# An encoder layer on one core: the rotation of q and k on VectorE, their turning amid other products, and a triangular substitution in three places

## The chip, the cores and the metric

The kernel runs on one core of a Trainium2 chip. The metric is device microseconds of one execution; lower is better. A core has TensorE (matrix products, PE in the views), VectorE (DVE), ScalarE (ACT), GpSimd (POOL), SyncE (SP, which here only issues DMAs) and 16 DMA engines that share its queues.

## The reference, cut to what matters

One layer of a hybrid encoder: x is 512 tokens by 1024. Two branches start from the same normalised h. Branch A is an RWKV-7 time mixing with a scan in both directions, branch B a differential attention. Both are gated and summed, then follow a feed-forward part and a second gate. The change touches branch B and a preparation of branch A's scan.

```python
q = partial_rope(q, cos, sin) * (DH ** -0.5)   # first 16 of each head's 64 are rotated
k = partial_rope(k, cos, sin)
...
def block(q_blk):
    s = jnp.einsum('bhcqd,bhckd->bhcqk', q_blk, kt).astype(f32)
    pr = jax.nn.softmax(s, axis=-1)
    pd = pr[:, :, 0] - lam * pr[:, :, 1]
    return jnp.einsum('bhqk,bhkv->bhqv', pd.astype(vt.dtype), vt)
...
o = o * lax.rsqrt(jnp.mean(o * o, axis=-1, keepdims=True) + SUBLN_EPS)
```

The scan of branch A (`state*w - ... + v*k`, 512 steps) is done in chunks of 64 tokens. Each chunk needs the inverse of a unit triangular 64x64 matrix; there are 128 of them (8 chunks, 8 heads, 2 directions), one to a partition.

## The kernel before

Every fp32 product is made of three products of rounded halves (`whi`/`wlo` of a weight, `hhi`/`hlo` of the activation), so a product is 3 matmuls a tile. A weight unit comes by DMA into `raw`; ScalarE rounds it to `whi`, VectorE (now and then GpSimd) forms `wlo`. The halves stand in a ring of four, the raw units in a ring of three.

The span goes through these stages: branch A's preparation, up to about 192 us; q, k and v of branch B (tiles `da`), up to 257; the attention loop, 17 turns, up to 320; the norm of its result, the corner blocks of the inverses and the branch's output product (`yb`), up to 382; branch A's scan, up to 486; then the output product, the feed-forward part and the last gate, up to the end.

**q, k, v.** For b = 0, 1, 2 (q, k, v) `dense_tm` makes two token tiles of 128 tokens at a time, 48 matmuls a pair. ScalarE scales each tile out of PSUM into `qk`; GpSimd rotates it (six operations of 128x64 for each token tile: L842 to L847, through the tile `rt`); TensorE turns it, 16 transposes of 128x128 into the four banks `qt` (L852); ScalarE and VectorE split each bank into halves (`qhl`, `kh`, `kl`).

**The loop.** Of each turn t: scores (`sc`), their largest value (`mx`), exponentials (`e`), the weighing of the two maps (GpSimd adds, VectorE scales by `s`), turning by TensorE (`tp`), the two halves of the turned tile (`turned_h` on ScalarE, `turned_l`, which is `pdTl` on VectorE), and the products with v (`ov`). Between them stand *fills*, three matmuls each: seven gates of eight fills into the banks `gA`, whose result `go` VectorE and ScalarE form, and then 32 fills of `yb`. There are two banks for gates: gate n+2 gets the bank of gate n once the `go` of gate n has been read out of it.

**The substitution.** `diag_blocks()` loads 2 MB into the tile `mi` (128 matrices, one to a partition) and inverts the two 32x32 diagonal blocks of each by 30 steps, s = 1 to 30. A step is two VectorE operations of 2*s*(31-s) elements a partition: 60, 116, 168, ... up to 480 at s = 15 and 16, and down again to 60. Then `mi` is stored to `td`, and four copies by ScalarE (`tr`) to `trd`. `corner_blocks()` loads both back (`u`, `bd`) and forms the off-diagonal block by four groups of 32 small matmuls (`iv`), which the scan needs.

**What sets the order.** `K(f, ...)` chains the operations of one engine in the order in which they are written; `chained` does so for TensorE. What isn't chained is put in order by a scheduler. `SUBS` says how many substitution steps are written ahead of q's, k's and v's products and in each turn of the loop, `CT` the turn in which the corner loads are written, `C0` the number of fills between the norm and the first `iv`.

Of the kernel before, what the change touches and what calls it, by code (L numbers as in the profile page):

```python
# [10 lines left out]
F32 = mybir.dt.float32  # L11
# [98 lines left out]
class Weights:  # L110
# [44 lines left out]
def tile_hybrid_encoder(ctx, tc, xT, wts, par, cst_a, cst_p, lor, lqk, nfin, out, dbg=None):  # L155
# [413 lines left out]
    AFS = [1, 1, 1, 1, 1, 1, 1, 1, 1, 1, 1, 1, 1, 2, 3, 3, 3]  # L569
# [47 lines left out]
    def diag_blocks():  # L617

        inv = pool("inv", side="right")
        mi = inv.tile([P, 2, H * (C + 1)], F32, name="mi")
        mif = mi.rearrange("u b x -> u (b x)")
        nc.sync.dma_start(mif[:, 0:C * C], md.rearrange("u s t -> u (s t)"))
        mfull = mif[:, 0:C * C].rearrange("u (s t) -> u s t", t=C)
        mb = mi[:, :, 0:H * C].rearrange("u b (s t) -> u b s t", t=C)
        tr = at.tile([P, H, H], F32, tag="pdTl", name="tr0", bufs=2)
        tmpo = inv.tile([P, 2 * 240], F32, name="tmpo")
        with tc.issue_after(W.last[0].ins):
            nc.scalar.activation(tr, mfull[:, 0:H, H:].rearrange("u s t -> u t s"), AF.Copy)  # L630
        nc.sync.dma_start(trd[:, 0], tr)
        for s in range(1, H - 1):
            n = H - 1 - s
            t_ = tmpo[:, 0:2 * s * n].rearrange("u (b i j) -> u b i j", b=2, j=n)
            with tc.issue_after(W.last[1].ins):
                nc.vector.tensor_tensor(t_, mb[:, :, 0:s, s:s + 1].broadcast_to([P, 2, s, n]),
                                        mb[:, :, s:s + 1, s + 1:H].broadcast_to([P, 2, s, n]), ALU.mult)
# [12 lines left out]
        nc.sync.dma_start(trd[:, 1], tr)  # L650
        inv.close_()
# [146 lines left out]
    for b in range(3):
        w = [W.next("intok", 1920 + 512 * b, k2) for k2 in range(4)]
        if b == 0:  # L800
            diag = diag_blocks()
        for _ in range(SUBS[b]):
            next(diag)
        if b < 2:
            qk = at.tile([P, 4, 8, 64], F32, tag="qk", name=f"qk{b}", bufs=1)
        pss_ = []
        for pair in range(2):
            for j in range(2):
                if pair == 0:
                    ps = psd.tile([P, 512], F32, tag="d", name=f"da{b}{j}")  # L810
                elif b < 2:
                    ps = psm.tile([P, 512], F32, tag="sc", name=f"da{b}{2 + j}", bufs=4)
                else:
                    ps = psm.tile([P, 512], F32, tag=("tp", "ov")[j], name=f"da{b}{2 + j}", bufs=1)
                pss_.append(ps)
            if b == 2 and pair == 1:
                for t in range(2):
                    scores(t)
                    exps(t)
                weigh(0)  # L820
            if last_pe is None:
                dense_tm(w, pss_[2 * pair:], 2 * pair, hhi, hlo)
            else:
                with tc.issue_after(last_pe.ins):
                    last_pe = dense_tm(w, pss_[2 * pair:], 2 * pair, hhi, hlo)
        for tt in range(4):
            ps = pss_[tt]
            if b < 2:
                nc.scalar.activation(qk[:, tt], ps.rearrange("p (h e) -> p h e", e=64), AF.Copy, scale=(rsq if b == 0 else rsx)[:, tt:tt + 1])
            else:  # L830
                nc.scalar.activation(vh[:, tt, :], ps, AF.Copy, scale=rsx[:, tt:tt + 1])
                nc.vector.scalar_tensor_tensor(vl[:, tt, :], ps, rsx[:, tt:tt + 1], vh[:, tt, :].bitcast(F32), ALU.mult, ALU.subtract)
        if b == 2:
            continue
        cos = ca[:, CA["cos"]:CA["cos"] + 32].rearrange("p (t e) -> p t e", e=8)
        sin = ca[:, CA["sin"]:CA["sin"] + 32].rearrange("p (t e) -> p t e", e=8)
        for tt in range(4):
            rt = at.tile([P, 4, 8, 8], F32, tag="rt", name=f"rt{b}{tt}", bufs=2)
            x1, x2 = qk[:, tt, :, 0:8], qk[:, tt, :, 8:16]
            cb = cos[:, tt, None, :].broadcast_to([P, 8, 8])  # L840
            sb = sin[:, tt, None, :].broadcast_to([P, 8, 8])
            nc.gpsimd.tensor_tensor(rt[:, 0], x1, cb, ALU.mult)  # L842
            nc.gpsimd.tensor_tensor(rt[:, 1], x2, sb, ALU.mult)
            nc.gpsimd.tensor_tensor(rt[:, 2], x2, cb, ALU.mult)
            nc.gpsimd.tensor_tensor(rt[:, 3], x1, sb, ALU.mult)
            nc.gpsimd.tensor_tensor(x1, rt[:, 0], rt[:, 1], ALU.subtract)
            nc.gpsimd.tensor_tensor(x2, rt[:, 2], rt[:, 3], ALU.add)  # L847
        dump("q" if b == 0 else "kq", qk)
        for hd in range(4):
            ps = psm.tile([P, T], F32, tag="sc", name=f"qt{b}{hd}", bufs=4)  # L850
            for tt in range(4):
                nc.tensor.transpose(ps[:, tt * P:(tt + 1) * P], qk[:, tt, 2 * hd:2 * hd + 2, :].rearrange("p h e -> p (h e)"), ident)  # L852
            for c in range(2):
                rows, other = slice(C * c, C * c + C), slice(C - C * c, P - C * c)
                dh = (qhl if b == 0 else kh2)[:, hd, c, :]
                nc.scalar.activation(dh[rows], ps[rows], AF.Copy)
                if b == 1:
                    nc.scalar.activation(dh[other], ps[rows], AF.Copy)
                dl = dh[other] if b == 0 else kl[rows, hd, c, :]
                nc.vector.tensor_tensor(dl, ps[rows], dh[rows].bitcast(F32), ALU.subtract)  # L860
# [52 lines left out]
    for t in range(NT + 1):  # L913
        if t > 2:
            values((t - 3) // 2, (0, 1) if t % 2 == 1 else (2, 3))
        if t + 3 < NT:
            scores(t + 3)
        fillk(AFS[t] if done < AFT else 0, True)
        if t > 0:
            turned_h(t - 1)  # L920
        if t + 2 < NT:
            exps(t + 2)
        if t + 1 < NT:
            weigh(t + 1)
# [557 lines left out]
```

## Time and profile before

| | |
|---|---|
| median of 3 runs | 973.64 us (965.7 to 975.59) |
| the profiled execution | 966.75 us, of which its span 964.8 us |
| TensorE busy | 888.8 us, 92% of the span |
| VectorE, ScalarE, GpSimd busy | 592.4, 450.5, 102.8 us |
| mean granted TensorE clock | 0.969 |

The span's busy time is 92% TensorE's. Granted clock is a share of 2.4 GHz. A row of a timeline gives start, duration, engine, line, operation and tiles; in brackets stands the idle time of that engine just before it and what ended it. L578 (and L667 in TensorE's rows) is the line in `K` (in `chained`), so operations recorded there are told apart by their tiles.

### The profile page before, as it was taken

How to read it: one execution, taken by the hardware profiler on the slowest of the kernel's cores; microseconds unless marked ns; L12 is line 12 of the kernel's file. 1: busy time of each engine (PE TensorE's matmuls, PEld its weight loads, DVE VectorE, ACT ScalarE, POOL GpSimd, SP SyncE). 2: the span in 40 equal slices, each digit the busy share in tenths (PEclk: the TensorE clock that was granted, in tenths of full speed). 3: DMA queues.
4: the chain of work that ended last, by engine and by line, in shares of the span. 5: the costliest groups of instructions: out<-in, count | busy, mean ns of one | idle time of the engine just before them, and what ended most of it. 6: DMA issues, size and time to landing. Idle time of an engine off the chain costs nothing.

```text
span 964.8 us, 14347 instructions
## 1 busy us (share of the span) xinstructions
PE 888.8 (92%) x5672; PEld 756.8 (78%) x5672; DVE 592.4 (61%) x885; ACT 450.5 (47%) x708; POOL 102.8 (11%) x139
## 2 busy tenths in 40 slices
PE   5899899987879998879999999999999999999996
PEld 4778777766767786668887788888888888888885
DVE  7766999667998632336889665554345335435453
ACT  7765555445578633213174454543234224313555
POOL 5000000144242141113200000000000000000000
PEclk9999999988989999889899999999999999999998
DMA  6343878742114468988524622333333332333512
GB/s 230 118 155 137 284 262 272 258 174 88 65 77 114 116 168 292 276 270 247 172 66 142 206 90 94 103 109 91 105 110 94 103 109 90 108 109 90 185 53 88
DMA packets 67859, 142.80 MB, mean 148 GB/s; under 512 B 26064, under 2 KB 28368, under 8 KB 65488
## 3 DMA queue, kind: packets, MB, share of 16 engines
q1 hardware_dynamic: 63696, 120.38, 38.5%
q0 software_dynamic: 4096, 21.50, 7.5%
q8 instruction: 45, 0.74, 0.3%
q14 instruction: 22, 0.18, 0.1%
HBM read 108.83 MB, written 33.03 MB: 147 GB/s over the span
## 4 chain that ended last, share of the span: by engine, by line
PE 61%; DVE 19%; DMA 7%; ACT 7%; issue 3%; POOL 2%; SPq 0%; DVEq 0%; ACTq 0%
PE f L247 11%; PE f L248 11%; PE f L246 11%; DMA ybt<-ybd 3%; PE gA L667 3%; DVE wlo L135 2%; DVE ga L520 2%; PE ss L1011 1%; DMA ybd<-yo 1%; PE wout L247 1%; PE wout L246 1%; PE wout L248 1%; DVE mx L578 1%; PE yy L1011 1%; PE yb L667 1%
## 5 line engine op out<-in xcount | busy, mean ns | idle before, releaser
L131 ACT ACTIVATE whi<-raw 128x1024 fp32r<-128x1024 f32 x134 | 141.4, 1056 | 282.8 <-PE f L247 182.8
L135 DVE TENSOR_TENSOR wlo<-raw,whi 128x1024 fp32r<-128x1024 f32 x131 | 163.2, 1247 | 51.6 <-ACT whi L131 51.4
L248 PE MATMUL f<-fh,wlo 128*128 128x512 f32 x256 | 97.2, 380 | 0.0
L246 PE MATMUL f<-fh,whi 128*128 128x512 f32 x256 | 97.1, 379 | 0.0
L247 PE MATMUL f<-fl,whi 128*128 128x512 f32 x256 | 97.1, 379 | 0.0
L247 PE MATMUL f<-h1l,whi 128*128 128x512 f32 x256 | 97.0, 379 | 0.0
L246 PE MATMUL f<-h1h,whi 128*128 128x512 f32 x256 | 97.0, 379 | 0.0
L248 PE MATMUL f<-h1h,wlo 128*128 128x512 f32 x256 | 97.0, 379 | 0.0
L1261 DVE TENSOR_TENSOR x<-x,f 128x512 f32<-128x512 f32 x32 | 22.0, 687 | 89.5 <-PE f L248 89.5
L1250 DVE SCALAR_TENSOR_TENSOR ft<-f,rf 128x512 f32<-128x512 f32 x32 | 22.1, 691 | 63.1 <-PE f L248 63.1
L246 PE MATMUL in<-hhi,whi 128*128 128x512 f32 x128 | 50.0, 391 | 6.6 <-ACT whi L131 6.6
L248 PEld LDWEIGHTS f<-h1h,wlo 128*128 128x128 f32 x256 | 48.4, 189 | 6.9
L247 PEld LDWEIGHTS f<-h1l,whi 128*128 128x128 f32 x256 | 48.4, 189 | 6.9
L246 PEld LDWEIGHTS f<-h1h,whi 128*128 128x128 f32 x256 | 48.4, 189 | 6.9
L246 PEld LDWEIGHTS f<-fh,whi 128*128 128x128 f32 x256 | 48.4, 189 | 6.8
L247 PEld LDWEIGHTS f<-fl,whi 128*128 128x128 f32 x256 | 48.4, 189 | 6.8
L248 PEld LDWEIGHTS f<-fh,wlo 128*128 128x128 f32 x256 | 48.4, 189 | 6.8
L247 PE MATMUL in<-hlo,whi 128*128 128x512 f32 x128 | 50.2, 392 | 1.5 <-DVE hlo L302 1.5
L248 PE MATMUL in<-hhi,wlo 128*128 128x512 f32 x128 | 49.9, 390 | 1.1 <-DVE wlo L135 1.1
L246 PE MATMUL da<-whi,hhi 128*128 128x512 f32 x96 | 38.3, 401 | 0.1
L247 PE MATMUL da<-wlo,hhi 128*128 128x512 f32 x96 | 37.9, 395 | 0.0
L248 PE MATMUL da<-whi,hlo 128*128 128x512 f32 x96 | 37.7, 392 | 0.0
(377 smaller groups left out, 1957.5 us busy)
## 6 DMA issues: line engine op xcount, KB each, us to landing
raw<-in_wts_dram SPq DMA_DIRECT2D x134, 512.0 KB, 3.5
gad<-ga SPq DMA_DIRECT2D x16, 1024.0 KB, 5.4
sga<-gad POOLq DMA_DIRECT2D x16, 1024.0 KB, 9.8
xs<-in_xT_dram SPq DMA_DIRECT2D x8, 256.0 KB, 5.8
ppd<-pps SPq DMA_DIRECT2D x2, 1024.0 KB, 5.5
md<-ga SPq DMA_DIRECT2D x32, 64.0 KB, 4.9
gates<-go SPq DMA_DIRECT2D x8, 256.0 KB, 2.9
mi<-md SPq DMA_DIRECT2D x1, 2048.0 KB, 9.9
```

What stands on the lines that cost most here:

```text
L131: a = nc.scalar.activation(hi, raw, AF.Copy)
L135: b = nc.vector.tensor_tensor(lo, raw, hi.bitcast(F32), ALU.subtract)
L246: nc.tensor.matmul(ps, lh, moved(rh), start=first, stop=False)
L247: nc.tensor.matmul(ps, lh, moved(rl), start=False, stop=False)
L248: return nc.tensor.matmul(ps, ll, moved(rh), start=False, stop=last)
L520: nc.vector.tensor_tensor(g_[:, :, P * hh:P * hh + P], aps[hh], mk[:, None, :].broadcast_to([P, 4, P]), ALU.mult)
L578: behind[e] = f(*args, **kw)
L667: last_pe = f(*args, **kw)
L1011: seq_last = nc.tensor.matmul(*args, **kw)
L1250: nc.vector.scalar_tensor_tensor(t_, ps, 0.0, rf, ALU.max, ALU.mult)
L1261: nc.vector.tensor_tensor(x[:, f, :], x[:, f, :], ps, ALU.add)
```

## The change

- The rotation is done by VectorE, six operations of 128x128 for two token tiles, chained by `K`: 24 operations in place of 48.
- k's first pair of token tiles is multiplied ahead of the turning of q; q's four banks are turned as one group of 16 between k's two pairs. k's turning stands amid v's products, in three pieces. v's last pair is split into two single tiles.
- The substitution's 30 steps: 7 behind the rotation of k's first pair, 3 behind that of its second, 2 amid v, 9 in the loop (turns 0 to 8), and the last 9 behind the norm. All are chained on VectorE.
- The first copy `tr` is chained on ScalarE ahead of step 12. The load of `mi` is issued by GpSimd in place of SyncE.
- The corner loads are written behind the substitution, so behind the norm (`CT` 17). There are 15 fills in place of 3 between the norm and the first `iv` (`C0`).

```diff
-    SUBS = [22, 0, 0, 1]
+    SUBS = [0, 7, 3, 9, 2]
-    C0 = 3
+    C0 = 15
-    CT = 15
+    CT = 17
...
-        nc.sync.dma_start(mif[:, 0:C * C], md.rearrange("u s t -> u (s t)"))
+        nc.gpsimd.dma_start(mif[:, 0:C * C], md.rearrange("u s t -> u (s t)"))
...
-        with tc.issue_after(W.last[0].ins):
-            nc.scalar.activation(tr, mfull[:, 0:H, H:].rearrange("u s t -> u t s"), AF.Copy)
-        nc.sync.dma_start(trd[:, 0], tr)
         for s in range(1, H - 1):
+            if s == 12:
+                K(nc.scalar.activation, tr, mfull[:, 0:H, H:].rearrange("u s t -> u t s"), AF.Copy)
+                nc.sync.dma_start(trd[:, 0], tr)
             n = H - 1 - s
...
-            nc.vector.tensor_tensor(mb[:, :, 0:s, s + 1:H], mb[:, :, 0:s, s + 1:H], t_, ALU.add)
+            K(nc.vector.tensor_tensor, mb[:, :, 0:s, s + 1:H], mb[:, :, 0:s, s + 1:H], t_, ALU.add)
...
+    def rotate(b, t2):
+        ts = slice(t2, t2 + 2)
+        rt = at.tile([P, 4, 2, 8, 8], F32, tag="rt", name=f"rt{b}{t2}", bufs=1)
+        x = qks[b][t2 // 2]
...
+        for i, (u, y) in enumerate(((x1, cb), (x2, sb), (x2, cb), (x1, sb))):
+            K(nc.vector.tensor_tensor, rt[:, i], u, y, ALU.mult)
+        K(nc.vector.tensor_tensor, x1, rt[:, 0], rt[:, 1], ALU.subtract)
+        K(nc.vector.tensor_tensor, x2, rt[:, 2], rt[:, 3], ALU.add)
...
+    rotate(0, 2)
+    substitute(SUBS[0])
+    wqkv = [W.next("intok", 1920 + 512, k2) for k2 in range(4)]
+    pk = pair("da1")
+    qkv(1, 0, pk)
+    for hd in range(4):
+        ps = bank(f"qt0{hd}")
+        transposed(0, hd, ps)
+        parts(0, hd, ps)
+        if hd == 1:
             for j in range(2):
...
+                scaled(1, j, pk[j])
+    rotate(1, 0)
+    substitute(SUBS[1])
+    ps = [bank(f"da1{2 + j}") for j in range(2)]
+    qkv(1, 2, ps)
+    for j in range(2):
+        scaled(1, 2 + j, ps[j])
+    rotate(1, 2)
+    substitute(SUBS[2])
...
-            for _ in range(SUBS[3]):
-                next(diag, None)
...
+        if t < SUBS[3]:
+            substitute(1)
...
+    for _ in diag:
+        pass
     if CT >= NT:
         next(corners)
     fillk(C0)
```

TensorE around the turning of q, before: the last of q's products (bank `da_1933`), then q's transposes (`qt`), bank by bank as the token tiles are ready.

```order
L246 MATMUL da_1933<-whi_1674,hhi 128x512
L247 MATMUL da_1933<-wlo_1675,hhi 128x512
L248 MATMUL da_1933<-whi_1674,hlo 128x512
L246 MATMUL da_1932<-whi_1674,hhi 128x512
L852 MATMUL qt_1871<-ca,qk_1738 128x128
L852 MATMUL qt_1880<-ca,qk_1738 128x128
L852 MATMUL qt_1889<-ca,qk_1738 128x128
L852 MATMUL qt_1871<-ca,qk_1738 128x128
L852 MATMUL qt_1880<-ca,qk_1738 128x128
```

After: the last of k's first pair (`da_1831`), q's 16 transposes, then k's second pair (`da_1946`).

```order
L246 MATMUL da_1831<-whi_1813,hhi 128x512
L247 MATMUL da_1831<-wlo_1814,hhi 128x512
L248 MATMUL da_1831<-whi_1813,hlo 128x512
L666 MATMUL qt_1880<-ca,qk_1661 128x128 x4
L666 MATMUL qt_1889<-ca,qk_1661 128x128 x4
L666 MATMUL qt_1900<-ca,qk_1661 128x128 x4
L666 MATMUL qt_1909<-ca,qk_1661 128x128 x4
L246 MATMUL da_1946<-whi_1677,hhi 128x512
L247 MATMUL da_1946<-wlo_1678,hhi 128x512
```

q's turning has moved from behind q's own products to behind 48 products of k.

VectorE behind the norm (`on`, `oT`), before: the halves of the norm's result, then gate results and weight halves.

```order
L971 TENSOR_TENSOR oT<-on_3039,oT 128x512
L971 TENSOR_TENSOR oT<-on_3046,oT 128x512
L969 SCALAR_TENSOR_TENSOR on_3060<-o__2274,one,rb_3057 128x512
L971 TENSOR_TENSOR oT<-on_3053,oT 128x512
L578 TENSOR_TENSOR go_3070<-gA_3007,rbs 128x512
L971 TENSOR_TENSOR oT<-on_3060,oT 128x512
L135 TENSOR_TENSOR wlo_3228<-raw_3226,whi_3227 128x1024
L578 TENSOR_SCALAR go_3070<-go_3070 128x512
L578 TENSOR_TENSOR go_3221<-gA_3081,rbs 128x512
```

After, at the same place: the substitution's last nine steps (`tmpo`, `mi`) begin amid the last `oT`, with two weight halves among them.

```order
L1022 TENSOR_TENSOR oT<-on_2979,oT 128x512
L578 TENSOR_TENSOR tmpo<-mi 128x396
L1022 TENSOR_TENSOR oT<-on_2986,oT 128x512
L578 TENSOR_TENSOR mi<-mi,tmpo 128x2x22x9
L135 TENSOR_TENSOR wlo_3086<-raw_3084,whi_3085 128x1024
L578 TENSOR_TENSOR tmpo<-mi 128x368
L578 TENSOR_TENSOR mi<-mi,tmpo 128x2x23x8
L578 TENSOR_TENSOR tmpo<-mi 128x336
L135 TENSOR_TENSOR wlo_3161<-raw_3159,whi_3160 128x1024
L578 TENSOR_TENSOR mi<-mi,tmpo 128x2x24x7
```

The gate results that came right behind the norm have moved behind the substitution. Its end on VectorE, before, inside the loop:

```order
L638 TENSOR_TENSOR mi<-mi,tmpo 128x2x29x2
L578 TENSOR_TENSOR go_2500<-gA_2287,rbs 128x512
L636 TENSOR_TENSOR tmpo<-mi 128x60
L638 TENSOR_TENSOR mi<-mi,tmpo 128x2x30
L578 TENSOR_SCALAR go_2500<-go_2500 128x512
L578 TENSOR_REDUCE mx_2531<-sc_2470 128x1
```

And after, behind the norm, with the gate results that followed `oT` before:

```order
L578 TENSOR_TENSOR tmpo<-mi 128x116
L578 TENSOR_TENSOR mi<-mi,tmpo 128x2x29x2
L578 TENSOR_TENSOR tmpo<-mi 128x60
L578 TENSOR_TENSOR mi<-mi,tmpo 128x2x30
L578 TENSOR_TENSOR go_3043<-gA_2933,rbs 128x512
L578 TENSOR_SCALAR go_3043<-go_3043 128x512
```

The last step, which the loop's `mx` followed, is now followed by the result of the fifth gate (`go_3043`) and then the sixth.

## Rows read from the trace of the kernel before

**Rows 1.** Busy time, TensorE clock and DMA share of three stretches.
```profile
core 0: us, PE busy (x) PEld busy (x) DVE busy (x) ACT busy (x) POOL busy (x), PEclk, DMA share, GB/s
...
200.00:210.00 10.00, 9.68 (x40) 8.21 (x40) 7.34 (x17) 6.42 (x9) 0.84 (x3) 0.74 0.35 134
...
230.00:240.00 10.00, 9.69 (x35) 8.27 (x36) 6.24 (x10) 7.45 (x13) 0.26 (x1) 0.71 0.05 19
...
270.00:280.00 10.00, 9.67 (x57) 8.16 (x55) 10.00 (x21) 9.18 (x24) 3.90 (x3) 1.00 0.01 2
```

**Rows 2.** Waits from 192 to 325 us (columns named in the first line).
```profile
engine line waited for: us in total, times, longest us
...
PE qt L852 <- POOL qk L847: 9.5, 6, 4.6
...
PE tp L667 <- DVE pdTl L578: 6.9, 7, 3.4
```

**Rows 3.** TensorE's timeline at the turning of q and of k (columns in line one).
```profile
start us, us, engine line op out<-in xcount [idle before <-releaser]
...
199.75 0.90 PE L852 MATMUL qt<-ca,qk 128*128 128x128 f32 x3 [2.20 <-POOL qk L847]
...
228.52 0.87 PE L852 MATMUL qt<-ca,qk 128*128 128x128 f32 x5 [4.56 <-POOL qk L847]
```

**Rows 4.** The rotation's tile rt (first row) and two rows of GpSimd's timeline.
```profile
L842 POOL TENSOR_TENSOR rt<-qk,ca x8: 313/320/990, 192.7 to 228.4; 128x64 f32<-128x64 f32 x8
...
265.87 1.27 POOL L578 TENSOR_TENSOR e<-e,e 128x512 f32<-128x512 f32 x1 [4.41 <-ACT e L578]
...
280.84 2.37 POOL L133 TENSOR_TENSOR wlo<-raw,whi 128x1024 fp32r<-128x1024 f32 x1 [1.92 <-ACT whi L131]
```

**Rows 5.** VectorE's timeline: substitution from 210 to 285 us, then the norm.
```profile
210.40 0.43 DVE L636 TENSOR_TENSOR tmpo<-mi 128x260 f32<-128x260 f32 x1
...
239.53 0.64 DVE L638 TENSOR_TENSOR mi<-mi,tmpo 128x476 f32<-128x476 f32 x1
...
266.06 1.36 DVE L636 TENSOR_TENSOR tmpo<-mi 128x260 f32<-128x260 f32 x1
...
267.47 0.68 DVE L578 TENSOR_TENSOR pdTl<-tp,pdTh 128x512 fp32r<-128x512 f32 x1
...
269.34 0.66 DVE L638 TENSOR_TENSOR mi<-mi,tmpo 128x260 f32<-128x260 f32 x1
...
280.96 2.38 DVE L638 TENSOR_TENSOR mi<-mi,tmpo 128x116 f32<-128x116 f32 x1
...
284.14 0.26 DVE L638 TENSOR_TENSOR mi<-mi,tmpo 128x60 f32<-128x60 f32 x1
...
333.67 2.06 DVE L969 SCALAR_TENSOR_TENSOR on<-o__2274,one,rb 128x512 f32<-128x512 f32 x3 [0.30 <-PE rb L667]
...
339.17 0.68 DVE L971 TENSOR_TENSOR oT<-on,oT 128x512 fp32r<-128x512 f32 x1
...
339.76 1.22 DVE L135 TENSOR_TENSOR wlo<-raw,whi 128x1024 fp32r<-128x1024 f32 x1
```

**Rows 6.** The chain of waits, from the last values to the first corner block.
```profile
319.92 1.46 PE ov L667 x12
...
326.30 6.67 PE gA L667 x30
...
335.03 2.14 PE gA L667 x9
...
337.17 1.99 PE iv L667 x64
```

**Rows 7.** SyncE's timeline: the stores and loads of the corner blocks.
```profile
284.43 0.33 SPq L642 DMA_DIRECT2D td<-mi  x1
...
290.92 3.15 SPq L883 DMA_DIRECT2D u<-td  x4
...
316.06 4.78 SPq L875 DMA_DIRECT2D bd<-trd  x8
```

**Rows 8.** Landing times in the views of tile mi, then of tile u.
```profile
DMA to landing us min/median/max: 6.5/8.2/9.9
...
DMA to landing us min/median/max: 3.7/4.0/4.4
```

**Rows 9.** TensorE's timeline in the branch's output products.
```profile
372.67 1.22 PE L667 MATMUL yb<-oT,whi 128*128 128x512 f32 x2 [4.10 <-ACT yo L782]
```

More of the change, by code (lines that the diff above doesn't have):

```diff
@@ L628, in diag_blocks @@
         tmpo = inv.tile([P, 2 * 240], F32, name="tmpo")
[L629 to L631 removed]
         for s in range(1, H - 1):
+            if s == 12:
+                K(nc.scalar.activation, tr, mfull[:, 0:H, H:].rearrange("u s t -> u t s"), AF.Copy)
+                nc.sync.dma_start(trd[:, 0], tr)
             n = H - 1 - s
             t_ = tmpo[:, 0:2 * s * n].rearrange("u (b i j) -> u b i j", b=2, j=n)
[L635 to L638 removed]
+            K(nc.vector.tensor_tensor, t_, mb[:, :, 0:s, s:s + 1].broadcast_to([P, 2, s, n]),
+              mb[:, :, s:s + 1, s + 1:H].broadcast_to([P, 2, s, n]), ALU.mult)
+            K(nc.vector.tensor_tensor, mb[:, :, 0:s, s + 1:H], mb[:, :, 0:s, s + 1:H], t_, ALU.add)
             yield
@@ L796, in fillk @@
                 gated()
[L798 to L807, printed above, removed]
-            for j in range(2):
[L809 to L860, printed above, removed]
@@ new lines, in tile_hybrid_encoder, with qkv, scaled @@
+    cos = ca[:, CA["cos"]:CA["cos"] + 32].rearrange("p (t e) -> p t e", e=8)
+    sin = ca[:, CA["sin"]:CA["sin"] + 32].rearrange("p (t e) -> p t e", e=8)
+    def qkv(b, tts, pss_):
+        nonlocal last_pe
+        if last_pe is None:
+            last_pe = dense_tm(wqkv, pss_, tts, hhi, hlo)
+        else:
+            with tc.issue_after(last_pe.ins):
+                last_pe = dense_tm(wqkv, pss_, tts, hhi, hlo)
+    def scaled(b, tt, ps):
+        K(nc.scalar.activation, qks[b][tt // 2][:, tt % 2], ps.rearrange("p (h e) -> p h e", e=64), AF.Copy, scale=(rsq if b == 0 else rsx)[:, tt:tt + 1])
@@ new lines, in transposed, with parts @@
+    def transposed(b, hd, ps):
+        for tt in range(4):
+            chained(nc.tensor.transpose, ps[:, tt * P:(tt + 1) * P], qks[b][tt // 2][:, tt % 2, 2 * hd:2 * hd + 2, :].rearrange("p h e -> p (h e)"), ident)
+    def parts(b, hd, ps):
+        for c in range(2):
+            rows, other = slice(C * c, C * c + C), slice(C - C * c, P - C * c)
+            dh = qhl[:, hd, c, :] if b == 0 else kh2[:, hd, c, :]
+            K(nc.scalar.activation, dh[rows], ps[rows], AF.Copy)
+            if b == 1:
+                K(nc.scalar.activation, dh[other], ps[rows], AF.Copy)
+            dl = dh[other] if b == 0 else kl[rows, hd, c, :]
+            K(nc.vector.tensor_tensor, dl, ps[rows], dh[rows].bitcast(F32), ALU.subtract)
@@ new lines, in substitute, with pair, bank @@
+    def substitute(n):
+        for _ in range(n):
+            next(diag, None)
+    def pair(name):
+        return [psd.tile([P, 512], F32, tag="d", name=f"{name}{j}") for j in range(2)]
+    def bank(name):
+        return psm.tile([P, T], F32, tag="sc", name=name, bufs=4)
+    qk = at.tile([P, 4, 8, 64], F32, tag="qk", name="qk0", bufs=1)
+    qks = [[qk[:, 0:2], qk[:, 2:4]], [at.tile([P, 2, 8, 64], F32, tag="pdTh", name=f"qk1{i}", bufs=2) for i in range(2)]]
+    wqkv = [W.next("intok", 1920, k2) for k2 in range(4)]
@@ new lines, in tile_hybrid_encoder @@
+    diag = diag_blocks()
+    ps = pair("da0")
+    qkv(0, 0, ps)
+    for j in range(2):
+        scaled(0, j, ps[j])
+    rotate(0, 0)
+    ps = [bank(f"da0{2 + j}") for j in range(2)]
+    qkv(0, 2, ps)
+    for j in range(2):
+        scaled(0, 2 + j, ps[j])
+    rotate(0, 2)
[8 more added lines that the diff above has]
+        if hd == 1:
+            for j in range(2):
+                scaled(1, j, pk[j])
@@ new lines, in tile_hybrid_encoder, with vparts @@
+    rotate(1, 0)
+    substitute(SUBS[1])
+    ps = [bank(f"da1{2 + j}") for j in range(2)]
+    qkv(1, 2, ps)
+    for j in range(2):
+        scaled(1, 2 + j, ps[j])
+    rotate(1, 2)
+    substitute(SUBS[2])
+    wqkv = [W.next("intok", 1920 + 1024, k2) for k2 in range(4)]
+    def vparts(tt, ps):
+        K(nc.scalar.activation, vh[:, tt, :], ps, AF.Copy, scale=rsx[:, tt:tt + 1])
+        K(nc.vector.scalar_tensor_tensor, vl[:, tt, :], ps, rsx[:, tt:tt + 1], vh[:, tt, :].bitcast(F32), ALU.mult, ALU.subtract)
@@ new lines, in tile_hybrid_encoder @@
+    pv = pair("da2")
+    qkv(2, 0, pv)
+    kts = [bank(f"qt1{hd}") for hd in range(2)]
+    for hd in range(2):
+        transposed(1, hd, kts[hd])
+        parts(1, hd, kts[hd])
+    for j in range(2):
+        vparts(j, pv[j])
+    substitute(SUBS[4])
+    pv = [psm.tile([P, 512], F32, tag=tag, name=f"da2{tag}", bufs=1) for tag in ("tp", "ov")]
+    qkv(2, 2, pv[0:1])
+    kts = pair("qt1")
+    transposed(1, 2, kts[0])
+    for t in range(2):
+        scores(t)
+        exps(t)
+    parts(1, 2, kts[0])
@@ L862, in corner_blocks @@
+    transposed(1, 3, kts[1])
+    vparts(2, pv[0])
+    weigh(0)
+    qkv(2, 3, pv[1:2])
+    parts(1, 3, kts[1])
+    vparts(3, pv[1])
     def corner_blocks():
```

7 lines of the change are left out of this document (3 added, 4 removed).

## The prediction

> **What bounds the kernel now.** I read the busy time by stretches first, then the waits around the change, then the timelines of the engines named there, and last the chain of waits up to the scan. TensorE is nearly always busy, but not at full clock: in the stretches from 200 and from 230 us its granted clock is 0.74 and 0.71, that is, part of the time at 1.2 and part at 2.4 GHz [rows 1]. Ahead of both stretches it had waited: its transposes of q and k waited 9.5 us in six pieces for GpSimd's rotation [rows 2], the longest pieces 2.20 and 4.56 us [rows 3]. So the rotation is on the path, and it costs its waits and some slow clock after them. From 270 to 280 us VectorE is busy all the time, the clock is full [rows 1], and TensorE's turning of the weighed maps waits for VectorE's `pdTl` (6.9 us in the loop) [rows 2]: there VectorE is the bound. Behind the last values the chain of waits is TensorE's alone, norm, fills, first corner block [rows 6]: there each matmul ahead of the corner counts, and VectorE has room. What the dense stages behind the scan do is the same in both kernels, so the change is worth what it moves the start of the scan. I set Z = 319.92 us, the start of the last values in the chain [rows 6], and ask how far Z moves, and how far the scan moves against Z.
>
> **Term 1, up to the loop.** Removed are the 9.5 us of waits. The two stretches at reduced clock lose at most 10 x (0.26 + 0.29) = 5.5 us against full clock [rows 1]. After the change, q's turning has k's first 48 products ahead of it. A matmul takes 0.216 us, from the fills of the chain: 30 take 6.67 and 9 take 2.14, so 21 more take 4.53 [rows 6]. 48 of them are 10.4 us; they cover q's second rotation, six VectorE operations of 128x128. Their cost is not in the trace; the nearest rows are a VectorE operation of 128x116 to 128x260, up to 0.43 us undisturbed [rows 5], and GpSimd's own 0.32 of half the width [rows 4]: some 0.35, so 2.1 us for six. q is covered. k's second rotation stands behind seven substitution steps and k's turning is covered by 48 of v's products, with less to spare. I take the 9.5 us as gone and half of the 5.5, as some small waits for banks and halves remain: **-12.3**. Bounds: -15.0 if all goes, and -6 if k's share of the waits, 5.5 of 9.5, comes back because VectorE's own queue (substitution, weight halves, rotation) is late in place of GpSimd's and only some of the clock is gained. The load of `mi` moves to GpSimd's queue; its 9.9 us to landing [rows 8] end near the first substitution step, which has cover in the products of k.
>
> **Term 2, the loop.** Nine steps stand in turns 0 to 8; eight of them lie behind the first `pdTl` (267.47 in the trace before [rows 5]), where VectorE is the bound, so VectorE's work adds to the path. An undisturbed operation on 260 elements takes 0.43 us and on 476 takes 0.64 [rows 5], so about 0.18 + 0.00097 a element. The eight steps have 3,696 elements and two operations each: 2 x (8 x 0.18 + 3.59) = 10.0 us. Before, there were nine small operations in that place, from 269.34 to 284.14, of which the rows show the first and the last [rows 5]; undisturbed they would be 2.9 us by the same line, and they took 6.4, since some stood beside GpSimd: 2.38 us for one of 116 elements, which began at 280.96 while GpSimd formed `wlo` from 280.84 to 283.21; 1.36 for 260 elements, beginning 0.19 us after GpSimd's `e` [rows 4, 5]. The `e` addition comes once a turn in both kernels and blocks one VectorE operation or another either way, so I keep that price as it is: 10.0 - 2.9 = **+7.1**. Bounds: +3.6 (10.0 - 6.4, no step blocked any more), +13.8 (each of eight turns pays one whole 1.27 us more: 10.0 + 10.2 - 6.4).
>
> The Trainium skill, "SBUF — State Buffer", section "Who interferes with whom", calls this an exclusive lock: a VectorE instruction with two SBUF inputs and a GpSimd instruction that reads SBUF block each other for a whole instruction. The two rows agree, since both operations end right behind GpSimd's. The rule speaks against moving the largest steps into the loop; it does not tell how many are hit, and it is the third rival below that takes it in full.
>
> **Term 3, from Z to the scan.** Before, the substitution ended at 284.14 [rows 5], `td` was stored at 284.43 and `u` loaded from 290.92 [rows 7], long ahead of the first corner block at 337.17 = Z + 17.3 [rows 6]. TensorE set that time, and 12 more fills ahead of the corner are 36 x 0.216 = 7.8 us, so with its operands ready the corner would start at Z + 25.0. After the change its operands are a serial path. VectorE's `on` begins at 333.67 = Z + 13.8 and the last `oT` ends at Z + 19.9 [rows 5]; without the gate result amid them, the first of the last nine steps starts at about Z + 18.8. The nine steps have 2,220 elements: 2 x (9 x 0.18 + 2.15) = 7.5 us. Two weight halves stand among them, 1.22 us each [rows 5], and the second waits for its ScalarE half, whose slot comes free only with the last matmul of the sixth gate: some 1.2 us. So the steps end near Z + 30. Queued behind them on VectorE is the fifth gate's result, which holds the bank of the seventh gate, so TensorE stands from about Z + 21.6 (30 of the 45 matmuls behind the norm) to Z + 30.7. Then the store of `td`, 6.5 us to landing [rows 8], to Z + 37; the four loads of `u`, 3.15 us to issue [rows 7] and 4.0 to landing [rows 8], to Z + 44, with the loads of `bd` in the same queue (4.78 for eight [rows 7]) up to Z + 46. First corner block at Z + 45 in place of Z + 25 with the fills counted as work done: TensorE is **20 us** later. Given back: the 36 matmuls of fills are no added work, they are taken from behind the corner, where TensorE stood 4.10 us for `yo` [rows 9] with some slow clock behind; fewer products are left there to wait. I take 2.5 of it: **+17.5**. Bounds: +7 (steps undisturbed, Z + 38.5 for the corner, 13.5 late, 6.3 given back) and +25.5 (store at 9.9, the longest landing of `mi` [rows 8], a longer wait for the weight half, nothing given back).
>
> **The sum.** -12.3 + 7.1 + 17.5 = +12.3 against the profiled execution's 966.75 us, so 979.0. That execution stands near the lower end of the three runs (965.7 to 975.59, median 973.64). For the median to come I start from the middle between the two, 970.2, which gives **982.5 us**. 1% of this kernel is 9.7 us, about what a measurement of it can tell from no change.
>
> **The rivals.**
>
> *Faster: the front of the loop gains more, and the tail hides.* Right ahead of the first `pdTl` a substitution step takes 1.36 in place of 0.43 us beside GpSimd [rows 5]; with two such steps gone from there the first `pdTl` could come 17 us earlier, as 15.0 of term 1 and two more. With the loop at its floor of +3.6 and the tail at +7 the sum is -6.4; with the loop at 0, because the steps fit the time in which VectorE waits for ScalarE (the chain would then pass through ScalarE's `pdTh`), it is -10, so some 960 from 970.2. It decides if the corner's operands are there within 7 us of the point where TensorE has finished its fills. For: the waits are plain rows, and their removal is sure. Against: VectorE is full at 270 to 280 [rows 1].
>
> *Even: gain and loss cancel.* Term 1 at -15, the loop at +3.6 and the tail at 11 to 15, if store and loads land faster than in my sum: -0.4 to +3.6, so 970 to 974 from the middle. For: the tail is a sum of eight steps, all but one with durations from another place of the program, and each may overlap more.
>
> *Slower still: GpSimd blocks the steps in full, and the turning of k isn't covered.* Each turn of the loop pays 1.27 us more (+13.8), and k's waits come back (-6 to -9): with the tail at +17.5 it is +22 to +25, so 992 to 995. It decides if half or more of the loop's steps take over 1.5 us. For: both rows of an overlap show a full block [rows 4, 5]. The lock of the skill's page, taken for each turn, is this case. Against: `s` and `e` operations on VectorE are hit before as well.
>
> That the change doesn't do what it says, so that TensorE still waits for the rotation, is part of the last: VectorE is 7.34 of 10 us busy in the stretch from 200 [rows 1] and could be as late as GpSimd was.
>
> **How the numbers follow.** Forecast (975 to 989): 0.42. Even: 0.26. Faster: 0.16. Slower still: 0.16. The range holds 8 in 10 if it reaches into both outer cases: from 961 (the faster rival's time) to 995 (the sum at the slow rival's end). The chances go by the change against the kernel before measured beside it: the forecast's +12.3 is 1.3% of 966.75. Slower by over 1% are the slow rival and most of the forecast, 0.54. Within 1%: 0.29. Faster by over 1%: 0.17.
>
> **What would show it.** Right: no wait of `qt` for a rotation above 1 us, the clock near 1.0 where it was 0.74 and 0.71; the first `pdTl` near 255; the loop's nine turns longer by some 7 us; the last `mi` near Z + 30; and between Z + 21 and Z + 46 TensorE nearly idle, once for `go` and once for `u`. Wrong: if the first corner block starts by Z + 32, term 3 is wrong and with it the sign; if `qt` waits for VectorE's rotation as long as for GpSimd's, term 1 is; if the loop is as long as before, term 2. A clock that falls behind the long idle time in the tail would add to the loss.

## The result, and the profile after

The changed kernel takes 983.96 us in the median (981.56 to 986.82), the kernel before 973.0; the ratio is 1.0136, 95% interval 1.0099 to 1.0174. The change makes the kernel 1.4% slower. The profiled execution has 981.56 us and a span of 979.6, which is 14.8 more than before; the medians differ by 11.0, since the profiled execution of the kernel before stands 6.3 us under its median and this one 2.4. The sums below go by the profiled executions.

The busy time by stretches of the changed kernel, columns as in [rows 1]:

```profile
core 0: us, PE busy (x) PEld busy (x) DVE busy (x) ACT busy (x) POOL busy (x), PEclk, DMA share, GB/s
...
200.00:210.00 10.00, 8.47 (x48) 7.41 (x47) 2.69 (x5) 2.90 (x5) 0.00 (x0) 1.00 0.30 123
...
230.00:240.00 10.00, 7.12 (x36) 6.00 (x35) 6.78 (x11) 7.73 (x11) 0.00 (x0) 1.00 0.00 0
...
250.00:261.00 11.00, 7.26 (x24) 5.20 (x24) 7.53 (x15) 8.21 (x16) 5.89 (x4) 0.84 0.31 100
...
340.00:350.00 10.00, 4.19 (x11) 3.41 (x12) 5.77 (x16) 1.22 (x2) 0.00 (x0) 0.66 0.61 244
...
350.00:360.00 10.00, 1.59 (x8) 1.00 (x6) 1.12 (x2) 0.63 (x1) 1.85 (x2) 0.82 0.93 204
```

The clock that was 0.74 and 0.71 behind the waits for the rotation is 1.00 in both stretches [rows 1]. Two new holes stand behind the norm: from 340 to 360 us TensorE is busy 5.8 of 20 us.

Its waits from 190 to 345 us:

```profile
engine line waited for: us in total, times, longest us
...
PE tp L666 <- DVE pdTl L578: 11.2, 11, 3.2
...
DVE mi L639 <- DMA mi<-md: 4.4, 1, 4.4
...
PE gA L666 <- DVE kl L578: 3.8, 1, 3.8
...
PE qt L666 <- DVE vl L578: 2.9, 1, 2.9
```

No transpose of q or k waits for a rotation any more, where it was 9.5 us [rows 2]. In their place stand 2.9 us for `vl` and 3.8 for `kl`, and the turning of the maps waits 11.2 for `pdTl` where it was 6.9 [rows 2].

VectorE's timeline in the changed kernel, to set beside [rows 5]:

```profile
261.46 0.68 DVE L578 TENSOR_TENSOR pdTl<-tp,pdTh 128x512 fp32r<-128x512 f32 x1
...
266.12 0.66 DVE L578 TENSOR_TENSOR mi<-mi,tmpo 128x480 f32<-128x480 f32 x1
...
292.79 0.68 DVE L578 TENSOR_TENSOR pdTl<-tp,pdTh 128x512 fp32r<-128x512 f32 x1
...
334.53 0.57 DVE L578 TENSOR_TENSOR tmpo<-mi 128x396 f32<-128x396 f32 x1
...
344.91 0.26 DVE L578 TENSOR_TENSOR mi<-mi,tmpo 128x60 f32<-128x60 f32 x1
...
345.07 0.68 DVE L578 TENSOR_TENSOR go<-gA,rbs 128x512 f32<-128x512 f32 x1
```

The first `pdTl` stands at 261.46, 6.0 us earlier than before [rows 5]. The last nine steps begin at 334.53 and end at 345.17, and the fifth gate's result comes right behind them. TensorE's timeline shows who waits for that:

```profile
345.81 0.80 PE L666 MATMUL gA<-hhi,whi 128*128 128x512 f32 x1 [8.14 <-DVE go L578]
...
357.96 0.39 PE L666 MATMUL iv<-u,bd 64*64 64x32 f32 x2 [6.76 <-DMA u<-td]
...
360.08 3.59 PE L666 MATMUL iv<-u,bd 64*64 64x32 f32 x62 [1.73 <-DMA u<-td]
...
395.80 0.70 PE L666 MATMUL yb<-oT,whi 128*128 128x512 f32 x2 [2.25 <-ACT yo L781]
```

8.14 us for `go`, then 6.76 and 1.73 for `u`. SyncE's timeline gives the path between, to set beside [rows 7]:

```profile
345.19 0.33 SPq L641 DMA_DIRECT2D td<-mi  x1
...
351.48 0.32 SPq L938 DMA_DIRECT2D u<-td  x1
...
354.65 1.97 SPq L938 DMA_DIRECT2D u<-td  x3
```

`td` is stored as soon as the last step has ended, and the loads of `u` are issued when that store has landed, 6.3 us later. Before, the same store stood at 284.43 [rows 7], 52.7 us ahead of the first corner block.

### The profile page after: what moved, and what is told of

Its sections match the earlier page's. It is cut to its first block, busy times and chain, and to the rows that moved or that the text cites. A ratio compares the mean times of both kernels' runs of the same rounds, so it can differ in the third digit from the quotient of the medians.

```text
span 979.6 us, 14314 instructions
## 1 busy us (share of the span) xinstructions
PE 890.2 (91%) x5672; PEld 756.7 (77%) x5672; DVE 588.7 (60%) x909; ACT 451.2 (46%) x708; POOL 81.8 (8%) x92
## 4 chain that ended last, share of the span: by engine, by line
PE 46%; DVE 6%; DMA 3%; ACT 3%; issue 1%; SPq 0%; DVEq 0%; ACTq 0%
PE f L247 11%; PE f L248 11%; PE f L246 11%; DMA ybt<-ybd 3%; PE yy L1064 1%; PE ss L1064 1%; PE wout L247 1%; PE wout L248 1%; PE wout L246 1%; PE al L1064 1%; PE pg L248 1%; PE pg L247 1%; PE pg L246 1%; DVE wlo L135 1%; PE gB L246 1%
## 5 line engine op out<-in xcount | busy, mean ns | idle before, releaser
L666 PE MATMUL gA<-hhi,whi 128*128 128x512 f32 x56 | 23.9, 426 | 12.0 <-DVE go L578 8.1
L246 PEld LDWEIGHTS in<-hhi,whi 128*128 128x128 f32 x128 | 25.0, 196 | 9.9 <-ACT whi L131 6.5
L246 PE MATMUL da<-whi,hhi 128*128 128x512 f32 x80 | 30.8, 387 | 1.7 <-DVE qhl L578 1.5
```

What stands on the lines that cost most here:

```text
L246: nc.tensor.matmul(ps, lh, moved(rh), start=first, stop=False)
L666: last_pe = f(*args, **kw)
```

## The experiments

The span is cut at four points, which each run's timelines show: the last product of v, the first `pdTl`, the norm's first matmul (`sso`, some 2.7 us behind Z), and the scan's first matmul (`al`). The column al - sso is the way from the norm to the scan. All are microseconds; runs are numbered as their labels (there is no run 5).

| kernel | last v | first pdTl | sso | last step ends | first iv | al | al - sso | span | ratio to before |
|---|---|---|---|---|---|---|---|---|---|
| before | 255.9 | 267.5 | 322.5 | 284.4 | 337.1 | 382.2 | 59.7 | 964.8 | |
| changed | 245.9 | 261.5 | 318.5 | 345.2 | 358.0 | 398.6 | 80.1 | 979.6 | 1.0136 |
| 1 tail in the loop, 3 fills | 247.6 | 263.3 | 327.3 | 317.3 | 342.9 | 398.5 | 71.2 | 977.9 | 1.0126 [1.0056, 1.0197] |
| 2 the same, 15 fills | 246.5 | 262.3 | 326.2 | 316.2 | 350.3 | 383.5 | 57.3 | 969.8 | 0.9967 [0.994, 0.9994] |
| 3 gate result first | 247.3 | 262.9 | 320.8 | 350.0 | 363.2 | 402.0 | 81.2 | 980.5 | 1.0123 [1.0076, 1.0169] |
| 4 40 fills | 245.6 | 261.2 | 318.2 | 344.8 | 375.4 | 406.8 | 88.7 | 980.1 | 1.0166 [1.0111, 1.0221] |
| 6 rotation on GpSimd | 250.2 | 265.8 | 322.8 | 349.5 | 362.1 | 403.0 | 80.2 | 986.1 | 1.0175 [1.0132, 1.0218] |
| 7 steps doubled | 246.4 | 263.8 | 332.8 | 359.5 | 372.3 | 412.5 | 79.7 | 994.0 | 1.0294 [1.0244, 1.0343] |
| 8 splits first | 247.0 | 262.6 | 320.9 | 349.0 | 361.9 | 402.8 | 82.0 | 984.4 | 1.0151 [1.0111, 1.0191] |
| 9 unchained, 22 early | 258.0 | 276.1 | 329.4 | 278.9 | 353.5 | 387.3 | 57.9 | 968.8 | 0.996 [0.9932, 0.9987] |
| 10 unchained, 7 and 15 | 252.6 | 274.2 | 327.9 | 291.0 | 350.3 | 384.4 | 56.5 | 967.2 | 0.9979 [0.9953, 1.0005] |
| 11 before, new tail alone | 255.9 | 262.5 | 315.6 | 342.3 | 355.3 | 396.6 | 81.0 | 978.7 | 1.0124 [1.0096, 1.0151] |
| 12 before, rotation on VectorE | 252.2 | 263.4 | 319.3 | 281.0 | 334.9 | 382.6 | 63.3 | 966.5 | 0.9986 [0.9958, 1.0014] |
| 13 the same, 15 fills | 252.6 | 263.7 | 318.9 | 280.5 | 342.9 | 376.9 | 58.0 | 957.7 | 0.9891 [0.9861, 0.9921] |

A part of a late start is made up inside the scan, or of an early one lost: from `al` to the end it is 582.6 us before, 581.0 in the changed kernel, 586.3 in run 2 and 573.3 in run 4. So a difference at `al` isn't yet one of the whole time.

The theory is that the serial path behind the norm (steps, store, loads, corner) is the loss, and that the front is a gain. The first rival is that the loss lies in the new order and the loop, the second that one of the two waits (the gate's bank) is a cost of its own.

**1 and 2. The last nine steps in the loop.** Steps, corner loads and, in run 1, the fills are put back ahead of Z.

```diff
         if t < SUBS[3]:
             substitute(1)
+        elif t < 13:
+            substitute(2)
+        elif t == 13:
+            for _ in diag:
+                pass
-    CT = 17
+    CT = 15
-    C0 = 15
+    C0 = 3
```

> The changed kernel, with the last nine substitution steps taken from behind the norm into turns 9 to 13 of the loop (two a turn), the corner loads back in turn 15 and 3 fills in place of 15 ahead of the first corner block. Theory (the tail): the serial path of steps, store and loads behind the norm is what costs; without it the corner starts at Z + 17 to 18 with no wait for u, the scan moves some 20 us ahead, and what is left of the change is its gain ahead of Z, about 4 us: 962 to 970 us, 0.6 to 0.3% under the kernel before. VectorE has room in turns 9 to 13, so Z moves by less than 3. Rival (the order of the products and the nine large steps in the loop cost the time): 978 us or more, with the waits in the tail gone and Z later.

Run 2 is the same with `C0 = 15`.

> As the run with the last nine steps in the loop, but with the 15 fills ahead of the corner kept. Theory (the tail): with its operands there, a later corner costs little, since the fills are work that has to be done anyway: within 3 us of the run with 3 fills. Rival (the 12 more fills ahead of the corner are the cost, because the scan's loads wait for the corner's store): 7 to 8 us more than that run.

Run 1 is 1.3% slower than the kernel before (profiled execution 979.65 us). The theory's 962 to 970 us are missed; the rival has its number (978 or more) and its later Z, but, as run 2 shows, not its cause. No wait for `go` is left and Z comes 8.9 us later (the steps do cost time in turns 9 to 13), but the corner stands at its place and the scan is still late. TensorE's timeline of run 1 tells why:

```profile
356.31 3.59 PE L666 MATMUL iv<-u,bd 64*64 64x32 f32 x62 [4.24 <-DMA bd<-trd]
...
389.05 1.22 PE L666 MATMUL yb<-oT,whi 128*128 128x512 f32 x2 [5.57 <-ACT yo L781]
```

With 3 fills the second half's `bd` isn't there when TensorE comes to it, and the products of `yb` wait 5.57 us for a store of `yo`. With 15 fills (run 2, 967.62 us) the wait for `bd` is gone and that for `yo` is 1.6 us, and the scan starts 57.3 us behind `sso`, where it was 80.1 in the changed kernel. Both expectations for run 2 missed: it should have come within 3 us of run 1 or 7 to 8 above it, and is 1.6% faster. So the 15 fills are no cost but a gain, and the 22.8 us less are the tail's price; 7.7 of them go back into Z. Of the 15.1 us by which the scan starts earlier than in the changed kernel, 9.8 reach the end of the span; where the rest goes is open. The rival that the new order and the steps of the loop cost the time falls with run 2, which keeps both and isn't slower than the kernel before.

**3. The gate's result ahead of the steps.**

```diff
+    fillk(5)
     for _ in diag:
         pass
-    C0 = 15
+    C0 = 10
```

> The changed kernel with 5 of the 15 fills written ahead of the last nine steps, so that the fifth gate's result stands ahead of them on VectorE and the seventh gate's bank is free in time. Theory (the corner's operands set the time, the bank only shows where TensorE stands first): the wait of 8.1 us for go vanishes, the wait for u grows by as much, and the steps end 1.1 us later: between -1 and +3 us against the changed kernel. Rival (the bank is a cost of its own): 8 us less.

982.63 us, al - sso 81.2 for 80.1. TensorE's timeline:

```profile
363.15 0.39 PE L666 MATMUL iv<-u,bd 64*64 64x32 f32 x2 [18.26 <-DMA u<-td]
...
365.57 3.59 PE L666 MATMUL iv<-u,bd 64*64 64x32 f32 x62 [2.03 <-DMA u<-td]
```

The wait for `go` is gone and that for `u` has grown from 8.5 to 20.3 us. The bank only showed where TensorE stood first; the second rival falls. The steps end 2.6 us later against `sso`, where 1.1 was expected.

**4. Fills in the hole.** `C0 = 40` in place of 15.

> The changed kernel with 40 fills in place of 15 ahead of the first corner block, so that 25 fills of yb (75 matmuls, 16 us) stand in the time in which TensorE waits for u. Theory (TensorE's idle time is the cost): the 6.8 and 1.7 us of waits for u and the slow clock behind them go, the 8.1 us for the bank stay: 6 to 11 us less than the changed kernel. Rival (the corner block's store and the scan's loads behind it set the start of the scan): no gain, or up to 7 us more, with the wait moved to the scan's first loads.

988.84 us: the rival's number. The wait for `u` is gone, and the scan's first matmul waits instead:

```profile
345.49 0.80 PE L666 MATMUL gA<-hhi,whi 128*128 128x512 f32 x1 [8.13 <-DVE go L578]
...
406.80 0.34 PE L1061 MATMUL al<-srv,sga 64*64 64x64 f32 x1 [13.95 <-DMA srv<-vd]
```

`srv` and `stt` are the scan's loads, which GpSimd issues behind the corner's store. They came late because the corner did: with 16 us of fills put into a hole of 8.5 us it starts at 375.4, which is 17.4 us later. TensorE's waits from `sso` to `al` add up to 29.8 us, for 20.4 in the changed kernel. So the run shows that 40 fills are too many, and that the chain from the corner through its store to the scan's loads is then the limit; whether a number that just fills the hole would gain isn't tested.

**6. The rotation on GpSimd, in the new order.** The same 24 operations, `nc.vector` replaced by `nc.gpsimd` in `rotate`.

> The changed kernel with the same 24 rotation operations on GpSimd in place of VectorE. Theory (the order gives the gain, since 48 products stand ahead of each turning): the rotation is covered on either engine, q's and k's turning wait under 1 us for it and the first pdTl moves by less than 1.5 us from 261.5: within 3 us of the changed kernel. Rival (the engine gives the gain): qt waits for GpSimd's qk by some 3 us or more at k's second half, and the first pdTl and the time come 3 to 6 us later.

987.52 us, first `pdTl` 4.3 us later, which is the rival's number, but not its mechanism: no `qt` waits for GpSimd. 2.5 of the 4.3 us are there ahead of the first rotation (q's first scaling by ScalarE starts at 195.48 for 193.02), and the wait of the `da` products for `qhl` has grown from 1.53 to 2.70, since the load of `mi`, which GpSimd issues, stands behind the rotation's first operations in its queue (198.52 for 192.43) and VectorE's `memset` of `mi`, ahead of its `qhl`, waits for it. For the waits the order is enough. Where the 2.5 us come from is open; in the runs whose order is the same up to there (1 to 4, 7) the last product of v alone differs by 2.0 us (245.6 to 247.6).

**7. The loop's steps doubled.**

```diff
+            if 13 <= s <= 21:
+                K(nc.vector.tensor_tensor, t_, mb[:, :, 0:s, s:s + 1].broadcast_to([P, 2, s, n]),
+                  mb[:, :, s:s + 1, s + 1:H].broadcast_to([P, 2, s, n]), ALU.mult)
```

> The changed kernel with each of the nine large steps of the loop doing its first operation twice (the same product written again, so nothing of the result changes): 9 operations of some 0.64 us, 5.8 us more work on VectorE, 8 of them behind the first pdTl. Theory (VectorE bounds the first turns of the loop): Z moves 4.5 to 6 us later and the time by 3 to 6 us. Rival (ScalarE or the weighing on GpSimd bounds those turns, and the steps stand in VectorE's waiting time): Z moves by less than 2 us.

998.17 us, Z 14.4 us later, more than twice the forecast. Eight turns behind the first `pdTl` take 43.4 us (263.8 to 307.2) for 31.3. VectorE is the bound (busy 41.7 of the 43.4 us), and the price of a step isn't its duration alone. VectorE's and GpSimd's timelines of one turn in this run:

```profile
269.37 1.34 DVE L578 TENSOR_TENSOR tmpo<-mi 128x480 f32<-128x480 f32 x2
...
270.75 1.62 DVE L578 TENSOR_TENSOR mi<-mi,tmpo 128x480 f32<-128x480 f32 x1
```

```profile
270.22 1.64 POOL L578 TENSOR_TENSOR e<-e,e 128x512 f32<-128x512 f32 x1 [3.39 <-ACT e L578]
```

The extra product lets GpSimd's `e` begin (270.22) ahead of the step's second operation, which then takes 1.62 in place of 0.66 us: 0.66 of work and 0.96 of block are 1.6 us a turn; over eight turns, seven of which are hit, this makes 12.0 of the 12.1 us.

**8. k's last splits ahead of the exponentials.**

```diff
     for t in range(2):
         scores(t)
-        exps(t)
     parts(1, 2, kts[0])
     transposed(1, 3, kts[1])
+    parts(1, 3, kts[1])
+    for t in range(2):
+        exps(t)
...
     qkv(2, 3, pv[1:2])
-    parts(1, 3, kts[1])
```

> The changed kernel with the splitting of k's third and fourth bank written ahead of the first two turns' exponentials, on ScalarE and VectorE, and the fourth turning ahead of them too. In the changed kernel v's last product stands 10.0 us earlier than before (245.9 for 255.9), but the first pdTl only 6.0. Theory (the order on ScalarE and VectorE between them, where the two splits wait behind exponentials, weight halves and largest values, holds the rest back): first pdTl 2 to 4 us earlier, near 258, and Z with it. Rival (ScalarE and VectorE are simply full there, in whatever order): less than 1 us, or later.

985.37 us; from the last product of v to the first `pdTl` 15.6 us, as in every run of the new order whose steps are chained (15.6 to 15.7), for 11.6 before. (In run 7 it is 17.4, since a doubled step lies in it.) The order within this stretch doesn't matter, and the rival has its number. That the two engines are full there isn't shown: from 250 to 261 us of the changed kernel VectorE is busy 7.53 and ScalarE 8.21 of 11 us. What sets the 15.6 us is open.

**9 and 10. The old substitution in the new front.** `diag_blocks` of the kernel before, unchained; 22 steps behind q's rotation (run 9) or 7 and 15 behind k's two (run 10), the rest one a turn; `CT = 15`, `C0 = 15`.

> The changed kernel's front and loop order with the substitution of the kernel before: its steps not chained, 22 written behind q's rotation, the rest one a turn in the loop, the load of mi on SyncE, corner loads in turn 15; the 15 fills ahead of the corner stay. Theory (the chained steps, nine large ones in the loop and nine behind the norm, are what costs; the front is a gain): steps end inside the loop near 280, Z at 312 to 316, no wait of TensorE for u or go behind the norm, scan at Z + 60 as in the run with the last nine steps in the loop and 15 fills: 955 to 963 us, faster than both kernels. Rival (with 22 steps early VectorE is late with the rotation of k and the splits, and the front's gain goes): first pdTl at 265 or later, 966 us or more.

> As the run with the unchained substitution (22 steps behind q's rotation, the rest one a turn, corner loads in turn 15, 15 fills), but with 7 steps behind the rotation of k's first pair and 15 behind that of its second. Theory (a step costs what VectorE is short of at its place; the place amid q and k delays rotation and splits most): the first pdTl comes 4 to 10 us earlier than the 276.1 of that run, Z near 318 to 323, the scan at Z + 60: 958 to 966 us. Rival (all places ahead of the scan cost the same, since VectorE and ScalarE are short everywhere up to Z): Z as in that run, near 327, within 3 us of 967.

967.12 and 968.42 us. The scan starts 57.9 and 56.5 us behind `sso`, but the first `pdTl` stands at 276.1 and 274.2, later than in either kernel. In the new front the early steps delay the rotation and the splits: in run 9 TensorE waits 1.7 us for a rotation and 4.4 for `qhl` (1.5 in the changed kernel). Run 9's rival was right on the front, and run 10's on the sum: two places with the same price.

**11. The new tail alone, in the kernel before.** Steps 22 to 30 are chained by `K`, the others are as before.

```diff
-    SUBS = [22, 0, 0, 1]
+    SUBS = [21, 0, 0, 0]
-    CT = 15
+    CT = 17
-    C0 = 3
+    C0 = 15
...
+    for _ in diag:
+        pass
     if CT >= NT:
         next(corners)
```

> The kernel before with the tail of the change alone: 21 substitution steps early as before, none in the loop, the last nine chained behind the norm, the corner loads behind them, 15 fills ahead of the corner; q, k and v in the old order, rotation on GpSimd. Theory (the serial path behind the norm costs some 20 us, whatever stands ahead): the scan starts at Z + 81 to 85 in place of Z + 62, and Z comes 3 to 7 us earlier than before, since VectorE does no steps in the loop: 984 to 992 us. Rival (the tail's loss comes from what the new order of the front does to it): the scan at Z + 70 or less, 975 us or less.

981.47 us, ratio 1.0124 for the whole change's 1.0136. TensorE's timeline has the same waits:

```profile
342.97 0.79 PE L672 MATMUL gA<-hhi,whi 128*128 128x512 f32 x1 [8.14 <-DVE go L578]
...
355.33 0.39 PE L672 MATMUL iv<-u,bd 64*64 64x32 f32 x2 [6.09 <-DMA u<-td]
```

al - sso is 81.0 for 59.7, and `sso` comes 6.9 us earlier, since no steps are left in the loop. The time is 2.5 us under the forecast's range; Z's gain lay at its upper end (6.9 of 3 to 7). The tail alone gives nearly the whole loss.

**12 and 13. The rotation alone, then with 15 fills.** In the kernel before, `nc.gpsimd` replaced by six `nc.vector` operations for two token tiles; in run 13 also `C0 = 15`.

> The kernel before with the rotation alone moved: 24 operations on VectorE for two token tiles each, in the old order of products, q turned behind its own products. Theory (the order gave the gain, not the engine): TensorE still waits for the rotation, some 2 to 4 us at q and as long at k, since VectorE has substitution steps in its queue: between -4 and +2 us against the kernel before. Rival (VectorE's faster rotation is the gain): the waits of qt under 2 us in all, the first pdTl at 262 or earlier, 967 us or less beside a kernel before at 972.

> The kernel before with the rotation on VectorE as in the run beside it, and 15 fills in place of 3 ahead of the first corner block; substitution, loads and product order as before. Theory (the later corner spares TensorE's waits behind it, as the two runs with the last nine steps in the loop showed with 15 and 3 fills): the scan starts some 2 us earlier against Z than with 3 fills, Z + 60 for Z + 62: 1 to 4 us less than the run with the rotation alone. Rival (the gain of 15 fills was due to late corner operands, which are early here): no difference, or up to 8 us more.

968.47 us (ratio 0.9986, no difference shown) and 959.2 us (0.9891). The waits of `qt` fall from 9.5 to 2.5 us in run 12 without any new order, and Z comes 3.2 us earlier; but with 3 fills the scan's start stays where it was. The 2.5 us are less than the theory's 4 to 8 and more than the rival's 2, and the first `pdTl`, at 263.4, misses the rival's 262. With run 6 beside it: the other engine alone takes most of the wait away, and so does the order alone. TensorE's timelines, of run 12 and then of run 13:

```profile
227.15 1.97 PE L851 MATMUL qt<-ca,qk 128*128 128x128 f32 x8 [2.20 <-DVE qk L846]
...
372.00 1.22 PE L667 MATMUL yb<-oT,whi 128*128 128x512 f32 x2 [5.04 <-ACT yo L782]
```

```profile
227.69 1.97 PE L851 MATMUL qt<-ca,qk 128*128 128x128 f32 x8 [3.54 <-DVE qk L846]
...
374.06 0.70 PE L667 MATMUL yb<-oT,whi 128*128 128x512 f32 x2 [2.26 <-ACT yo L782]
```

The wait of `yb` for `yo` is 5.04 us with 3 fills (4.10 before [rows 9]) and 2.26 with 15, and al - sso falls from 63.3 to 58.0. Of the 3.6 us by which run 12's way to the scan is longer than that of the kernel before, 0.9 are this wait; the rest is time in which TensorE works, at a granted clock of 0.79 from 330 to 335 us and 0.73 from 370 to 382.5. Run 13 is 9.3 us faster than run 12, more than twice the 1 to 4 us that were expected; 5.7 of the 8.8 us between their spans lie ahead of the scan, the others are open. It is faster than both kernels and the fastest of all runs, in the old order of products. 15 fills in the kernel before, without the rotation on VectorE, weren't run.

## Why the prediction was right, and where its terms were not

The forecast was 982.5 us and +12.3 against the profiled execution; measured are 983.96 and +14.8, or +11.0 between the medians. The sign and the cause, term 3, were right. That the sum came so close was luck: term 1 was off by 6.3 us one way and term 2 by 5.1 the other.

- **Term 1, -12.3, measured -6.0.** The waits for the rotation and the slow clock behind them went as forecast, though 2.9 us for `vl` and 1.5 for `qhl` stand in their place: v's last product stands 10.0 us earlier. The step that failed is the one that lets this arrive at the first `pdTl`: 4.0 of the 10.0 are lost between the two, and the first `pdTl` stands at 261.5 and not near 255. Half of k's splits now lie behind v's products, which may be the reason and isn't shown; run 8 shows that another order there gains nothing.
- **Term 2, +7.1, measured +2.0** (first to ninth `pdTl`, 31.3 for 29.4 us), under the lower bound of 3.6. The step that failed is the price of the block "as it is": in the changed kernel no step of the loop is blocked (0.66 us for 480 elements); GpSimd's `e` is, at 1.64 for 1.27 [rows 4], and in the waits of these turns no engine stands for an `e` that was. (In most turns ScalarE does the scaling by `s`, and GpSimd's `e` is the difference of the two maps.) The steps also push the small operation that forms `s`, one element a partition, behind the end of `e`, which blocked four of eight of them before. VectorE's timelines, before and then changed:

```profile
272.22 1.24 DVE L578 SCALAR_TENSOR_TENSOR s<-s,one,s 128x1 f32<-128x1 f32 x1
```

```profile
264.70 0.22 DVE L578 SCALAR_TENSOR_TENSOR s<-s,one,s 128x1 f32<-128x1 f32 x1
```

The first stands beside GpSimd's `e` (272.11 to 273.43). In the stretch the eight of them took 4.8 us before and take 1.8 now. So the steps bring 10.15 us of work, and 6.4 of the old steps and 3.05 of `s` leave; the prediction's lower bound counted the first two only. One gate result, 1.55 us for 0.43, adds 1.1: +1.8 by these terms. Run 7 shows the other order, and what it costs.
- **Term 3, +17.5, measured +20.4** (al - sso, 80.1 for 59.7). The steps ended at Z + 29.5 (315.7 for Z), forecast 30; TensorE stood 8.1 us for the bank, forecast 9.1; the corner ran from Z + 42 and 44, forecast 45. Run 11 shows the term by itself (+21.3), run 2 its absence. Of the 2.5 us "given back" 1.85 came (the wait for `yo` is 2.25 for 4.10). The step that was mis-sized is the slow clock behind the idle time, which the prediction named and left out of the sum. Between `sso` and `al` stand the same matmuls in both kernels: TensorE's waits there are 20.4 us for 4.4, which is 16.0 of the 20.4, and the other 4.4 us are time in which it works, at a granted clock of 0.50 from 358 to 365 us and 0.64 from 345.8 to 351.2.
- **The rest.** The scan and what follows took 1.6 us less (span less al, 581.0 for 582.6). -6.0 + 2.0 + 20.4 - 1.6 = +14.8, the difference of the spans.

The faster rival needed the corner's operands within 7 us of TensorE's fills; TensorE stood idle for 8.1 and 8.5 us before they were there. The even rival had the tail at 11 to 15, and it is 20.4. The slower rival's test, half of the steps over 1.5 us, failed in the changed kernel.

## What to carry to other kernels

Work whose result goes through a store and a load before the next stage can use it must end early, whatever engine has room late: the same nine steps cost some 20 us behind the norm and 8 in the loop. An idle engine shows where a path is late, not what the path is: freeing the first wait (run 3) gained nothing, and more work in the hole than it holds (run 4) moved the wait to the next load. And a gain at the end of one stage is to be followed to the next shared point before it is booked.

## What the runs showed that was not expected

Which of two engines pays for a collision is set by a few tenths of a microsecond. GpSimd's `e` at 266.28 of the changed kernel:

```profile
266.28 1.64 POOL L578 TENSOR_TENSOR e<-e,e 128x512 f32<-128x512 f32 x1 [1.76 <-ACT e L578]
```

It began 0.16 us behind VectorE's second operation of the step (266.12) and took 1.64 us, and VectorE 0.66; in run 7 it began 0.53 us ahead of that operation, which took 1.62. The Trainium skill, "SBUF — State Buffer", section "Who interferes with whom", says: "Issue order, not op shape, decides who blocks." The two runs agree; in run 7, though, GpSimd's `e` took 1.64 as well, having begun while the repeated product was still running.

The idle time in the tail also costs clock: behind the wait for `u` the 62 corner matmuls take 3.59 us in the changed kernel where 64 took 1.99 before [rows 6] (a group's 32 matmuls stand in the trace as 64), and the granted clock is 0.50, the level of 1.2 GHz, in run 3's stretch from 350 to 360 us, in which TensorE does nothing.
